# Placing SBUF buffers at multiples of 512 bytes, with a set offset for each block of weights

## The chip, the cores and the metric

The kernel runs on one core of a Trainium2 chip. The metric is the device time of one execution in microseconds (us); a number given for a kernel is the median of several executions. Within an execution, times are taken from the hardware profiler's trace, counted from the start of its span.

## The reference

One decoder layer for 256 tokens of width 1024, all in float32:

```python
h = rms_norm(x); proj = h @ w_in            # q, k, v | c_q, c_kv, k_r | 2 x 1024 gate columns
o_a = moba_attention(rope(q), rope(k), v) @ w_branch_a      # 8 heads x 64; at 256 tokens plain causal
q = rms_norm(c_q) @ w_uq; kv = rms_norm(c_kv) @ w_ukv       # low-rank attention, 8 heads, 64 + 32 rope
o_b = mla_attention(q, kv, rope(k_r)) @ w_branch_b
merged = sigmoid(g_a) * o_a + sigmoid(g_b) * o_b
x = x + rms_norm(merged @ w_out)
x = x + rms_norm(relu(rms_norm(x) @ w_up)**2 @ w_down)      # hidden width 4096
```

## The kernel before

Every float32 product is made of three TensorE matmuls in the type float32r: each operand is split into a high part (ACT copies it, rounded) and a low part (DVE subtracts), and `mm3` (lines 177 to 182) adds high x high, low x high and high x low into one PSUM tile. Line 179 issues the first of the three and line 182 the other two. The order of TensorE's instructions is the order of the program text; the other engines' order is set by the same text and a few explicit dependencies.

A matmul has two SBUF operands. The **stationary** one (128 columns, 512 bytes of each partition) is loaded into the array by a weight load, which the profile lists as PEld; the **moving** one (256, 288, 384 or 512 columns) streams through. In the trace a matmul stands as `out<-moving,stationary`. Two helpers use `mm3`:

- `a_chunk` (lines 265 to 277): the activations `xt` or `ct` are stationary and a block of weights moves, 512 columns as a rule. It makes q, k, v, and the latent projections cq (384 columns) and ckv (288).
- `b_tile` (lines 279 to 285): a block of weights is stationary, 128 columns at a time, and activations of 256 tokens move. It makes the gates (16 blocks `g{m}_{br}`, line 539), the branch projections (8 blocks `br{m}`, line 621) and the up projection (14 pairs `up{2i}`, lines 857 to 862). `nope` (line 564) does the same for the blocks uq and uk.

`unit` (line 162) loads one block of up to 1024 columns into a `raw` tile by a DMA of SP's queue, and splits it into the tiles `whi` and `wlo`, which rotate through 5 buffers each. In the second half `load` and `split` (lines 647 to 666) do the same with 2048 columns: tiles `u_hi`, `u_lo` for up, `t` or `b` for down.

The stages, in order of time: q, cq and ckv; k with the rotary work; v with the latent work; both attentions, woven with gate tiles; the branch projections `br`; the output projection `out` (`mix`, line 718, 96 matmuls with weights moving); the first part of up, with the split x1 stationary and `t` moving (line 765); then a loop over pairs (line 857) in which 48 matmuls of up alternate with 21 or 24 of down (`down`, line 846). Down's stationary operand is the squared activation, `m_hi` or `m_lo`, and its moving operand a block of 512 columns of `t`, `b` or `u`. Down has 204 matmuls on `t`, 99 on `b` and 60 on `u` (the last 24 with 256 columns).

Tiles come from pools that are stacked upwards from the low end of a partition's bytes, or (side="right") downwards from the high end, in the order in which they are first asked for. So the start of a tile follows from the sizes of those before it. In the program as built the starts, taken modulo 512, are these (all buffers of one name have the same remainder; a slice of 128 columns is 512 bytes and a step of 256 columns 1024, so slices keep the remainder):

```
tile                         before    after
xt_hi, xt_lo, x1_hi, x1_lo     320       0
whi, wlo (blocks of unit)      480       0 + the block's offset
o_hi, o_lo                     384       0
mg_hi, mg_lo, ct_hi, ct_lo     480       0
u_hi, u_lo                     480       0 + the block's offset
t_hi, t_lo                     320       0
b_hi, b_lo, m_hi, m_lo         480       0
```

The code that sets the position of a block of weights:

```python
hi = wts.tile([P, UNIT], F32R, name="whi", tag="whi")[:, :width]          # line 168
hi = mlp(f"{tag}h").tile([P, size], F32R, name=f"{tag}_hi", tag=f"{tag}h")[:, :n]   # line 651
```

The load of the first up block (`upA0`, line 665, in `mix`) goes into a `raw_u` buffer that lies where tiles of the attention half lay, so it waits for their last readers or writers.

Of the kernel before, what the change touches and what calls it, by code (L numbers as in the profile page):

```python
# [133 lines left out]
def block_kernel(ctx: ExitStack, tc: tile.TileContext, x, xt, pos_col, g_post_in, weights, out):  # L134
    nc = tc.nc
    table, _ = _block_table()

    keep = ctx.enter_context(tc.tile_pool(name="keep", bufs=1))

    first_half, attention_part = ExitStack(), ExitStack()  # L140
    late, wts = (first_half.enter_context(tc.tile_pool(name=n, bufs=b, side="right"))
# [17 lines left out]
    last_split = []  # L159


    def unit(key, hi=None, lo=None, behind=None):


        off, width = table[key]
        raw = wts.tile([P, UNIT], F32, name="raw", tag="raw", bufs=6)[:, :width]
        if hi is None:
            hi = wts.tile([P, UNIT], F32R, name="whi", tag="whi")[:, :width]
            lo = wts.tile([P, UNIT], F32R, name="wlo", tag="wlo")[:, :width]
        nc.sync.dma_start(raw, weights[off:off + P * width].rearrange("(p c) -> p c", c=width))  # L170
        ops = nc.scalar.activation(hi, raw, AF.Copy), nc.vector.tensor_tensor(lo, raw, hi, op=OP.subtract)  # L171
        for op, first in zip(ops, behind or ()):
            after(op, first)
        last_split[:] = ops
        return hi, lo

    def mm3(ps, a_hi, a_lo, b_hi, b_lo, first, last, a_lo_last=False):
# [22 lines left out]
    inv_freq = att.tile([P, 16], F32, name="inv_freq")  # L200
    for i in range(16):
        nc.gpsimd.memset(inv_freq[:, i:i + 1], INV_FREQ[i])
    mask = att.tile([P, 3 * P], F32, name="mask")
    nc.gpsimd.memset(mask, 0.0)
    for c in (0, 2):
        m = mask[:, c * P:(c + 1) * P]
        nc.gpsimd.affine_select(m, m, pattern=[[-1, P]], base=0, channel_multiplier=1,
                                compare_op=OP.is_ge, fill=NEG)


    stat = keep.tile([P, 128], F32, name="stat")
# [53 lines left out]
    def a_chunk(ps, key, n, x_hi, x_lo, nk, starts, before=None):  # L265

        starts = list(starts) + [nk]
        for k0, k1 in zip(starts, starts[1:]):
            if before is not None:
                before(k0, k1)  # L270
            hi, lo = (u.rearrange("p (k n) -> p k n", n=n) for u in unit(f"{key}{k0}"))
            for k in range(k0, k1):
                for t in range(NT):
                    tok = slice(t * P, (t + 1) * P)
                    mm3(ps[t], x_hi[:, k, tok], x_lo[:, k, tok], hi[:, k - k0], lo[:, k - k0],
                        k == 0, k == nk - 1)
                yield 6 * n / 2.4
# [25 lines left out]
    ctx.enter_context(tc.manual_schedule(engines={nc.tensor.engine}))  # L303


    zeros = att.tile([P, 512], BF16, name="zeros")
    nc.vector.memset(zeros, 0.0)
    first = stat_cols(1)
    nc.scalar.activation(first, zeros[:, :1], AF.Copy)
# [147 lines left out]
    def attention(br, products, v_of, scale):  # L457


        ranges = ((0, P), (P, 3 * P))  # L460
        probs, pts = {}, {}

        def softmax(h, sp):
            sm = att.tile([P, 3 * P], F32, name="sm", tag="sm", bufs=3)
            st = att.tile([P, 6], F32, name="st", tag="st", bufs=4)
            pr = att.tile([P, 3 * P], F32, name="pr", tag="pr", bufs=4)
            for t, (a, b) in enumerate(ranges):
                nc.vector.tensor_tensor_reduce(sm[:, a:b], sp[t], mask[:, a:b], scale=-scale, scalar=3.0e38,
                                               op0=OP.add, op1=OP.min, accum_out=st[:, t:t + 1])
                last_exp[0] = nc.scalar.activation(pr[:, a:b], sm[:, a:b], AF.Exp, bias=st[:, t:t + 1], scale=-1.0,  # L470
                                     accum_out=st[:, 2 + t:3 + t])
            nc.vector.reciprocal(st[:, 4:6], st[:, 2:4])
            for t, (a, b) in enumerate(ranges):
                nc.vector.tensor_scalar(pr[:, a:b], pr[:, a:b], st[:, 4 + t:5 + t], None, op0=OP.mult)
            probs[h] = pr

        def turned(h):
            pp = wk_tile()
            transposes(pp, [probs[h][:, c * P:(c + 1) * P] for c in range(3)])
            pts[h] = att.tile([P, 3 * P], F32, name="pt", tag="pt", bufs=3)  # L480
            nc.scalar.copy(pts[h], pp[:, :3 * P])
# [53 lines left out]
    def gate_tiles():  # L535
        for m in range(KD):
            ps = acc_tile()
            for br in range(2):
                yield from b_tile(ps[:, br * S:(br + 1) * S], unit(f"g{m}_{br}"), xt_hi, xt_lo, KD)
            nc.vector.tensor_tensor(gate(m), ps.rearrange("p (b s) -> p b s", b=2),  # L540
                                    rstd_row[:, None, :].to_broadcast([P, 2, S]), op=OP.mult)
            gates_done[0] += 1
# [7 lines left out]
    def latent_work():  # L550
# [25 lines left out]
            nc.scalar.copy(dst[:, 1:4:2], psv[64:128])  # L576

        for i in range(2):
            yield from nope(unit(f"uq{i}_0"), 256, 0, range(3), qMT[0:NOPE, 4 * i:4 * i + 4])
        u = unit("uk0")  # L580
        for i in range(2):
            yield from nope(u, 512, i, (3, 4), kMT[0:NOPE, 4 * i:4 * i + 4])
        ps = [acc_tile() for _ in range(NT)]
# [34 lines left out]
    gates_up_to(1)  # L618
    left = KD - gates_done[0]
    for m in range(KD):  # L620
        u = unit(f"br{m}")
        ps = wk_tile()
        for br in range(2):
            run(b_tile(ps[:, br * S:(br + 1) * S], u, o_hi[:, br], o_lo[:, br], 4, base=4 * br))
            sig = nc.scalar.activation(gate(m)[:, br], gate(m)[:, br], AF.Sigmoid, bias=col(B_GATE, br * KD + m))
            after(sig, last_exp[0])
        pr = att.tile([P, 2 * S], F32, name="mp", tag="mp", bufs=2)
        nc.vector.tensor_tensor(pr, ps, gate(m).rearrange("p b s -> p (b s)"), op=OP.mult)
        sm = att.tile([P, S], F32, name="ms", tag=("ra", "rb")[m % 2])
# [14 lines left out]

        return mlp0 if tag in ("raw_u", "raw_d", "th", "tl", "m0n", "r") else mlp1[0]

    def split(src, tag, behind=(), parts=1):

        n = src.shape[-1]
        size = {"b": 3 * 512}.get(tag, PAIR)  # L650
        hi = mlp(f"{tag}h").tile([P, size], F32R, name=f"{tag}_hi", tag=f"{tag}h")[:, :n]
        lo = mlp(f"{tag}l").tile([P, size], F32R, name=f"{tag}_lo", tag=f"{tag}l")[:, :n]
        for i in range(parts):
            c = slice(i * n // parts, (i + 1) * n // parts)
            ops = nc.scalar.activation(hi[:, c], src[:, c], AF.Copy), \  # L655
                nc.vector.tensor_tensor(lo[:, c], src[:, c], hi[:, c], op=OP.subtract)  # L656
# [61 lines left out]
    def mix():  # L718


        us = [unit(f"out{k}") for k in range(KD)]
        up_a[:] = [split(load(f"upA{k}", tag), "t") for k, tag in ((0, "u"), (4, "d"))]
        pieces = [[acc_tile() for n in range(2)] for t in range(NT)]

# [132 lines left out]
    for i in range(WARM // 2, n_pairs):  # L857
        ps = wk_tile()
        behind = {2: (turned[0, 1], turned[1, 0]), 3: (turned[1, 1],)}.get(i, ())
        w = split(load(f"up{2 * i}", "u"), "u", behind, max(len(behind), 1))  # L860
        for j in range(2):
            run(b_tile(ps[:, j * S:(j + 1) * S], w, x1_hi, x1_lo, KD, base=j * KD))
            if i == WARM // 2 and j == 0:
# [76 lines left out]
```

## Time and profile before

| | |
|---|---|
| median of 3 executions | 371.86 us (371.44 to 371.88) |
| the profiled execution | 371.55 us |
| its span, first to last instruction | 369.8 us |
| mean granted TensorE clock | 0.994 |
| busy in the span | PE 97%, PEld 87%, DVE 81%, ACT 67%, POOL 2% |

The profile is of one execution. PE is a busy time in which matmuls overlap each other, so a busy share of 97% does not say at what pace the matmuls go; the pace is the distance from one matmul's start to the next one's, called the gap below. DVE is VectorE, ACT ScalarE, POOL GpSimd, SP the engine that issues the DMAs.

### The profile page before, as it was taken

How to read it: one execution, taken by the hardware profiler on the slowest of the kernel's cores; microseconds unless marked ns; L12 is line 12 of the kernel's file. 1: busy time of each engine (PE TensorE's matmuls, PEld its weight loads, DVE VectorE, ACT ScalarE, POOL GpSimd, SP SyncE). 2: the span in 40 equal slices, each digit the busy share in tenths (PEclk: the TensorE clock that was granted, in tenths of full speed). 3: DMA queues.
4: the chain of work that ended last, by engine and by line, in shares of the span. 5: the costliest groups of instructions: out<-in, count | busy, mean ns of one | idle time of the engine just before them, and what ended most of it. 6: DMA issues, size and time to landing. Idle time of an engine off the chain costs nothing.

```text
span 369.8 us, 6081 instructions
## 1 busy us (share of the span) xinstructions
PE 359.7 (97%) x2319; PEld 321.5 (87%) x2319; DVE 298.0 (81%) x555; ACT 248.8 (67%) x375; POOL 6.5 (2%) x29
## 2 busy tenths in 40 slices
PE   8999999999999999999999999999999999999992
PEld 4699888989998999998879998889999888999881
DVE  4898898985766576796686999999989979978556
ACT  6889569996758755647289966767747766545422
POOL 6000000000000000000000000000000000000000
PEclk9999999999999999999999999999999999999997
DMA  7987763455434356574804756456564447330002
GB/s 252 403 327 244 258 205 106 125 218 152 136 96 133 113 172 178 179 268 179 334 3 165 268 194 252 180 193 228 228 217 161 170 177 284 131 115 0 2 0 113
DMA packets 15036, 66.20 MB, mean 179 GB/s; under 512 B 1696, under 2 KB 2208, under 8 KB 10912
## 3 DMA queue, kind: packets, MB, share of 16 engines
q1 hardware_dynamic: 14688, 65.30, 50.5%
q10 hardware_dynamic: 288, 0.52, 0.4%
q8 instruction: 18, 0.29, 0.3%
q14 instruction: 10, 0.08, 0.1%
q0 software_dynamic: 32, 0.00, 0.0%
HBM read 64.77 MB, written 1.05 MB: 178 GB/s over the span
## 4 chain that ended last, share of the span: by engine, by line
PE 91%; DVE 4%; DMA 2%; ACT 1%; SPq 1%; issue 1%; DVEq 0%; ACTq 0%
PE acc L182 30%; PE wk L182 27%; PE acc L179 15%; PE wk L179 13%; PE wk L368 3%; DMA raw<-in_weights 2%; PE wk L488 1%; PE wk L520 1%; ACT sq L242 1%; DVE y L898 1%; PE wk L489 1%; DVE x_lo L714 0%; PE wk L519 0%; SPq L255 0%; DVE y L685 0%
## 5 line engine op out<-in xcount | busy, mean ns | idle before, releaser
L171 DVE TENSOR_TENSOR wlo<-raw,whi 128x1024 fp32r<-128x1024 f32 (+4 forms) x58 | 65.7, 1139 | 20.3 <-ACT whi L171 20.3
L171 ACT ACTIVATE whi<-raw 128x1024 fp32r<-128x1024 f32 (+4 forms) x58 | 57.2, 992 | 28.6 <-PE acc L182 13.3
L179 PE MATMUL wk<-x_hi,u_hi 128*128 128x256 f32 x224 | 63.3, 283 | 0.0
L182 PE MATMUL wk<-x_lo,u_hi 128*128 128x256 f32 x224 | 63.3, 282 | 0.0
L182 PE MATMUL wk<-x_hi,u_lo 128*128 128x256 f32 x224 | 62.9, 281 | 0.0
L655 ACT ACTIVATE u_hi<-raw_u 128x2048 fp32r<-128x2048 f32 (+1 forms) x17 | 30.9, 1816 | 28.0 <-PE wk L182 27.9
L656 DVE TENSOR_TENSOR u_lo<-raw_u,u_hi 128x2048 fp32r<-128x2048 f32 (+1 forms) x17 | 36.8, 2162 | 10.6 <-ACT u_hi L655 10.2
L182 PEld LDWEIGHTS wk<-x_lo,u_hi 128*128 128x128 f32 x224 | 42.1, 188 | 0.6
L182 PEld LDWEIGHTS wk<-x_hi,u_lo 128*128 128x128 f32 x224 | 42.5, 190 | 0.0
L179 PEld LDWEIGHTS wk<-x_hi,u_hi 128*128 128x128 f32 x224 | 42.0, 187 | 0.6
L179 PE MATMUL acc<-xt_hi,whi 128*128 128x256 f32 x128 | 37.8, 295 | 0.0
L182 PE MATMUL acc<-xt_hi,wlo 128*128 128x256 f32 x128 | 36.1, 282 | 0.0
L182 PE MATMUL acc<-xt_lo,whi 128*128 128x256 f32 x128 | 36.0, 281 | 0.0
L656 DVE TENSOR_TENSOR t_lo<-t,t_hi 128x2048 fp32r<-128x2048 f32 x11 | 25.2, 2288 | 2.0 <-ACT t_hi L655 1.9
L805 ACT ACTIVATE m_hi<-m 128x896 fp32r<-128x896 f32 (+1 forms) x16 | 14.6, 917 | 15.9 <-DVE m L801 13.6
L179 PEld LDWEIGHTS acc<-xt_hi,whi 128*128 128x128 f32 x128 | 24.0, 188 | 1.1 <-issue 1.0
L182 PEld LDWEIGHTS acc<-xt_lo,whi 128*128 128x128 f32 x128 | 24.2, 189 | 0.1
L182 PEld LDWEIGHTS acc<-xt_hi,wlo 128*128 128x128 f32 x128 | 24.1, 188 | 0.0
L655 ACT ACTIVATE t_hi<-t 128x2048 fp32r<-128x2048 f32 x11 | 21.0, 1911 | 1.8 <-PE acc L182 1.1
L656 DVE TENSOR_TENSOR b_lo<-raw_d,b_hi 128x1536 fp32r<-128x1536 f32 x11 | 19.2, 1749 | 0.0
L806 DVE TENSOR_TENSOR m_lo<-m,m_hi 128x896 fp32r<-128x896 f32 (+1 forms) x16 | 16.6, 1044 | 2.5 <-ACT m_hi L805 2.5
L182 PE MATMUL acc<-t_lo,m_hi 128*128 128x512 f32 x46 | 18.3, 398 | 0.0
(254 smaller groups left out, 927.9 us busy)
## 6 DMA issues: line engine op xcount, KB each, us to landing
raw<-in_weights SPq DMA_DIRECT2D x44, 512.0 KB, 3.6
raw_u<-in_weights SPq DMA_DIRECT2D x17, 1024.0 KB, 5.0
raw_d<-in_weights SPq DMA_DIRECT2D x15, 1024.0 KB, 4.9
raw<-in_weights SPq DMA_DIRECT2D x7, 384.0 KB, 6.9
raw<-in_weights SPq DMA_DIRECT2D x4, 256.0 KB, 4.5
x_sb<-in_x SPq DMA_DIRECT2D x2, 512.0 KB, 8.1
g_post<-in_g_post SPq DMA_DIRECT2D x2, 512.0 KB, 5.4
raw<-in_weights SPq DMA_DIRECT2D x2, 432.0 KB, 6.8
```

The lines of the kernel that those rows point to most:

```text
L171: ops = nc.scalar.activation(hi, raw, AF.Copy), nc.vector.tensor_tensor(lo, raw, hi, op=OP.subtract)
L179: nc.tensor.matmul(ps, a_hi, b_hi, start=first, stop=False)
L182: nc.tensor.matmul(ps, a, b, start=False, stop=last and i == 1)
L242: return nc.scalar.activation(sq[:, :src.shape[-1]], src, AF.Square, scale=scale, accum_out=accum)
L368: nc.tensor.transpose(ps[:n, i * P:(i + 1) * P], b, ident)
L488: nc.tensor.matmul(o[:, 0:S], v_of(0, h), pts[h][:, 0:S], start=True, stop=False)
L489: nc.tensor.matmul(o[:, P:S], v_of(1, h), pts[h][:, S:S + P], start=False, stop=True)
L520: nc.tensor.matmul(sp[:, P:3 * P], q[:, P:2 * P], k, start=True, stop=True)
L655: ops = nc.scalar.activation(hi[:, c], src[:, c], AF.Copy), \
L656: nc.vector.tensor_tensor(lo[:, c], src[:, c], hi[:, c], op=OP.subtract)
L805: nc.scalar.activation(hi, m[:, used], AF.Copy)
L806: nc.vector.tensor_tensor(lo, m[:, used], hi, op=OP.subtract)
```

## The change

Three things are done. The large tiles are moved to multiples of 512 bytes, by fillers (`edge`, `pad_kr`, `pad_o`, a wider `stat`) and by letting small tiles share buffers (`zeros` with `rb`, `mp` with `sm`; `mask` loses a third, since both score ranges can read the same causal block). The tiles of weights get 512 bytes more, and each block starts at its own offset in them: a gate block at 32(2m+br) bytes, a k block at 64 k0, a v block at 64 k0 + 64, an out block at 32(2k+1), an up block at 32 i, the blocks br, uq and uk at 192; all others at 0. The arguments `hi`, `lo` and `behind` of `unit`, which no call used, are gone.

```diff
+ROW, SKEW = 512, 192
+    ctx.enter_context(tc.tile_pool(name="edge", bufs=1, side="right")).tile([P, 120], F32, name="edge")
-    def unit(key, hi=None, lo=None, behind=None):
+    def unit(key, skew=0):
         off, width = table[key]
         raw = wts.tile([P, UNIT], F32, name="raw", tag="raw", bufs=6)[:, :width]
-        if hi is None:
-            hi = wts.tile([P, UNIT], F32R, name="whi", tag="whi")[:, :width]
-            lo = wts.tile([P, UNIT], F32R, name="wlo", tag="wlo")[:, :width]
+        hi, lo = (wts.tile([P, UNIT + ROW // 4], F32R, name=n, tag=n)[:, skew // 4:skew // 4 + width]
+                  for n in ("whi", "wlo"))
...
-    mask = att.tile([P, 3 * P], F32, name="mask")
+    mask = att.tile([P, 2 * P], F32, name="mask")
-    for c in (0, 2):
-        m = mask[:, c * P:(c + 1) * P]
-        nc.gpsimd.affine_select(m, m, ...
+    nc.gpsimd.affine_select(mask[:, P:], mask[:, P:], ...
-    stat = keep.tile([P, 128], F32, name="stat")
+    stat = keep.tile([P, 176], F32, name="stat")
-            hi, lo = (... for u in unit(f"{key}{k0}"))
+            hi, lo = (... for u in unit(f"{key}{k0}", 64 * k0 + 64 * (key == "v") if key in "kv" else 0))
-    zeros = att.tile([P, 512], BF16, name="zeros")
+    zeros = att.tile([P, 512], BF16, name="zeros", tag="rb")
+    att.tile([P, 48], F32, name="pad_kr")
+    att.tile([P, 64], F32, name="pad_o")
-                nc.vector.tensor_tensor_reduce(sm[:, a:b], sp[t], mask[:, a:b], ...
+                nc.vector.tensor_tensor_reduce(sm[:, a:b], sp[t], mask[:, 2 * P - (b - a):], ...
-                yield from b_tile(ps[:, br * S:(br + 1) * S], unit(f"g{m}_{br}"), xt_hi, xt_lo, KD)
+                yield from b_tile(ps[:, br * S:(br + 1) * S], unit(f"g{m}_{br}", 32 * (2 * m + br)), xt_hi, xt_lo, KD)
-            yield from nope(unit(f"uq{i}_0"), ...
-        u = unit("uk0")
+            yield from nope(unit(f"uq{i}_0", SKEW), ...
+        u = unit("uk0", SKEW)
-        u = unit(f"br{m}")
+        u = unit(f"br{m}", SKEW)
-        pr = att.tile([P, 2 * S], F32, name="mp", tag="mp", bufs=2)
+        pr = att.tile([P, 2 * S], F32, name="mp", tag="sm", bufs=3)
-    def split(src, tag, behind=(), parts=1):
+    def split(src, tag, behind=(), parts=1, skew=0):
-        size = {"b": 3 * 512}.get(tag, PAIR)
-        hi = mlp(f"{tag}h").tile([P, size], F32R, ...)[:, :n]
-        lo = mlp(f"{tag}l").tile([P, size], F32R, ...)[:, :n]
+        size = {"b": 3 * 512, "u": PAIR + ROW // 4}.get(tag, PAIR)
+        hi = mlp(f"{tag}h").tile([P, size], F32R, ...)[:, skew // 4:skew // 4 + n]
+        lo = mlp(f"{tag}l").tile([P, size], F32R, ...)[:, skew // 4:skew // 4 + n]
-        us = [unit(f"out{k}") for k in range(KD)]
+        us = [unit(f"out{k}", 32 * (2 * k + 1)) for k in range(KD)]
-        w = split(load(f"up{2 * i}", "u"), "u", behind, max(len(behind), 1))
+        w = split(load(f"up{2 * i}", "u"), "u", behind, max(len(behind), 1), 32 * i)
```

No instruction changes its place on PE, ACT, DVE or SP; POOL has one AFFINE_SELECT less at its start. Two DMAs wait for something else, because the buffers now lie over other tiles of the first half. On SP's queue, at the end of `mix`'s loads, stood before:

```order
L170 DMA raw<-in_weights 128x1024 [waits DMAHW5_49,DVE_49]
L665 DMA raw_u<-in_weights 128x2048 [waits PE_49,Pool_49]
L665 DMA raw_d<-in_weights 128x2048 [waits PE_49]
L665 DMA raw_u<-in_weights 128x2048 [waits DMAHW6_49,DVE_49,Pool_49]
L665 DMA raw_u<-in_weights 128x2048 [waits DMAHW7_49,DMAHW4_49,DVE_49]
```

and with the change:

```order
L171 DMA raw<-in_weights 128x1024 [waits DMAHW5_49,DVE_49]
L663 DMA raw_u<-in_weights 128x2048 [waits DVE_49,PE_49,Pool_49]
L663 DMA raw_d<-in_weights 128x2048 [waits PE_49]
L663 DMA raw_u<-in_weights 128x2048 [waits DMAHW6_49,Pool_49]
L663 DMA raw_u<-in_weights 128x2048 [waits DMAHW7_49,DMAHW4_49,DVE_49]
```

The first `raw_u` is upA0. It now waits also for DVE, and the count it waits for is that of the last `mg_lo` (m = 7, line 632 before). The third load, up4, no longer waits for DVE (a count reached three DVE steps earlier, at the last `mp`).

## Rows read from the trace of the kernel before

**Rows 1.** The page: busy time, share of the span and instructions of each engine, and the chain that ended last by engine.

```profile
PE 359.7 (97%) x2319; PEld 321.5 (87%) x2319; DVE 298.0 (81%) x555; ACT 248.8 (67%) x375; POOL 6.5 (2%) x29
PE 91%; DVE 4%; DMA 2%; ACT 1%; SPq 1%; issue 1%; DVEq 0%; ACTq 0%
```

**Rows 2.** The waits of PE over the whole span: who waited for whom, us in total, times, longest us.

```profile
PE wk L312 <- DVE stat L636: 1.3, 1, 1.3
PE acc L182 <- DVE x_lo L714: 0.9, 1, 0.9
PE wk L182 <- DVE wlo L171: 0.5, 1, 0.5
PE wk L179 <- ACT whi L171: 0.2, 1, 0.2
```

**Rows 3.** Three stretches: start and end, us, busy us (and instructions) of PE, PEld, DVE, ACT, POOL, granted PE clock, DMA share, GB/s.

```profile
0.00:20.00 20.00, 18.02 (x64) 11.85 (x65) 13.12 (x27) 14.47 (x23) 6.47 (x29) 1.00 0.90 333
220.00:240.00 20.00, 20.00 (x130) 18.10 (x129) 19.74 (x19) 14.10 (x12) 0.00 (x0) 1.00 0.59 215
280.00:300.00 20.00, 20.00 (x134) 18.37 (x133) 17.43 (x17) 12.81 (x11) 0.00 (x0) 1.00 0.60 211
```

**Rows 4.** The timeline of PE in one turn of the loop over pairs: start us, duration us, instruction. The first and last of 12 matmuls of down on t, of 48 of up, and of 9 of down on b.

```profile
246.35 0.40 PE L179 MATMUL acc<-t_hi,m_hi 128*128 128x512 f32 x1
...
248.93 0.40 PE L182 MATMUL acc<-t_lo,m_hi 128*128 128x512 f32 x1
249.17 0.28 PE L179 MATMUL wk<-x_hi,u_hi 128*128 128x256 f32 x1
...
254.81 0.28 PE L182 MATMUL wk<-x_hi,u_lo 128*128 128x256 f32 x1
254.92 0.39 PE L179 MATMUL wk<-b_hi,m_hi 128*128 128x512 f32 x1
...
256.78 0.39 PE L182 MATMUL acc<-b_lo,m_hi 128*128 128x512 f32 x1
```

**Rows 5.** The same view: the first and the last three of 48 matmuls of a gate tile.

```profile
135.47 0.28 PE L179 MATMUL acc<-xt_hi,whi 128*128 128x256 f32 x1
...
140.87 0.28 PE L179 MATMUL acc<-xt_hi,whi 128*128 128x256 f32 x1
140.98 0.29 PE L182 MATMUL acc<-xt_lo,whi 128*128 128x256 f32 x1
141.11 0.28 PE L182 MATMUL acc<-xt_hi,wlo 128*128 128x256 f32 x1
```

**Rows 6.** The same view: the first and last of 120 matmuls of the branch projections br3 to br7.

```profile
149.47 0.28 PE L179 MATMUL wk<-o_hi,whi 128*128 128x256 f32 x1
...
163.44 0.28 PE L182 MATMUL wk<-o_hi,wlo 128*128 128x256 f32 x1
```

**Rows 7.** The same view: the first of the out projection, its 60th (the first to use the low part of block out7), and its 93rd, the last before transposes come between.

```profile
163.55 0.39 PE L179 MATMUL acc<-whi,mg_hi 128*128 128x512 f32 x1
...
176.93 0.39 PE L182 MATMUL acc<-wlo,mg_hi 128*128 128x512 f32 x1
...
184.41 0.39 PE L182 MATMUL acc<-wlo,mg_hi 128*128 128x512 f32 x1
```

**Rows 8.** The same view, near the end of the loop: the first and last of 36 matmuls of down on u.

```profile
351.36 0.40 PE L179 MATMUL acc<-u_hi,m_hi 128*128 128x512 f32 x1
...
359.33 0.39 PE L182 MATMUL acc<-u_lo,m_hi 128*128 128x512 f32 x1
```

**Rows 9.** The same view: the first and last of 48 matmuls each of cq (384 columns), ckv (288) and k (512).

```profile
18.75 0.34 PE L179 MATMUL acc<-whi,xt_hi 128*128 128x384 f32 x1
...
26.89 0.34 PE L182 MATMUL acc<-wlo,xt_hi 128*128 128x384 f32 x1
27.07 0.29 PE L179 MATMUL acc<-whi,xt_hi 128*128 128x288 f32 x1
...
33.33 0.30 PE L182 MATMUL acc<-wlo,xt_hi 128*128 128x288 f32 x1
33.46 0.40 PE L179 MATMUL wk<-whi,xt_hi 128*128 128x512 f32 x1
...
44.48 0.39 PE L182 MATMUL wk<-wlo,xt_hi 128*128 128x512 f32 x1
```

**Rows 10.** The timeline of DVE around the load of upA0: the last mg_lo, and the low parts of upA0 and of block out7.

```profile
165.96 0.42 DVE L632 TENSOR_TENSOR mg_lo<-ms,mg_hi 128x256 fp32r<-128x256 f32 x1
...
171.92 2.29 DVE L656 TENSOR_TENSOR t_lo<-raw_u,t_hi 128x2048 fp32r<-128x2048 f32 x1 [0.58 <-ACT t_hi L655]
174.13 1.22 DVE L171 TENSOR_TENSOR wlo<-raw,whi 128x1024 fp32r<-128x1024 f32 x1
```

**Rows 11.** The timeline of SP's queue: the issues of upA0 and upA4.

```profile
158.15 0.38 SPq L665 DMA_DIRECT2D raw_u<-in_weights  x1
163.63 0.33 SPq L665 DMA_DIRECT2D raw_d<-in_weights  x1
```

**Rows 12.** All loads of line 665 in the span: time from issue to landing.

```profile
DMA to landing us min/median/max: 4.7/4.9/7.3
```

**Rows 13.** The timeline of ACT: the high parts of upA0 and of out7.

```profile
169.98 1.90 ACT L655 ACTIVATE t_hi<-raw_u 128x2048 fp32r<-128x2048 f32 x1
171.79 1.05 ACT L171 ACTIVATE whi<-raw 128x1024 fp32r<-128x1024 f32 x1
```

More of the change, by code (lines that the diff above doesn't have):

```diff
@@ L159, in block_kernel @@
     last_split = []
-    def unit(key, hi=None, lo=None, behind=None):
+    def unit(key, skew=0):
         off, width = table[key]
         raw = wts.tile([P, UNIT], F32, name="raw", tag="raw", bufs=6)[:, :width]
-        if hi is None:
-            hi = wts.tile([P, UNIT], F32R, name="whi", tag="whi")[:, :width]
-            lo = wts.tile([P, UNIT], F32R, name="wlo", tag="wlo")[:, :width]
+        hi, lo = (wts.tile([P, UNIT + ROW // 4], F32R, name=n, tag=n)[:, skew // 4:skew // 4 + width]
+                  for n in ("whi", "wlo"))
         nc.sync.dma_start(raw, weights[off:off + P * width].rearrange("(p c) -> p c", c=width))
[L171 to L174, printed above, removed]
+        last_split[:] = nc.scalar.activation(hi, raw, AF.Copy), nc.vector.tensor_tensor(lo, raw, hi, op=OP.subtract)
         return hi, lo
@@ L202, in block_kernel @@
         nc.gpsimd.memset(inv_freq[:, i:i + 1], INV_FREQ[i])
-    mask = att.tile([P, 3 * P], F32, name="mask")
+    mask = att.tile([P, 2 * P], F32, name="mask")
     nc.gpsimd.memset(mask, 0.0)
-    for c in (0, 2):
-        m = mask[:, c * P:(c + 1) * P]
-        nc.gpsimd.affine_select(m, m, pattern=[[-1, P]], base=0, channel_multiplier=1,
-                                compare_op=OP.is_ge, fill=NEG)
-    stat = keep.tile([P, 128], F32, name="stat")
+    nc.gpsimd.affine_select(mask[:, P:], mask[:, P:], pattern=[[-1, P]], base=0, channel_multiplier=1,
+                            compare_op=OP.is_ge, fill=NEG)
+    stat = keep.tile([P, 176], F32, name="stat")
     used = [0]
@@ L270, in a_chunk @@
                 before(k0, k1)
-            hi, lo = (u.rearrange("p (k n) -> p k n", n=n) for u in unit(f"{key}{k0}"))
+            hi, lo = (u.rearrange("p (k n) -> p k n", n=n) for u in unit(f"{key}{k0}", 64 * k0 + 64 * (key == "v") if key in "kv" else 0))
             for k in range(k0, k1):
@@ L467, in softmax @@
             for t, (a, b) in enumerate(ranges):
-                nc.vector.tensor_tensor_reduce(sm[:, a:b], sp[t], mask[:, a:b], scale=-scale, scalar=3.0e38,
+                nc.vector.tensor_tensor_reduce(sm[:, a:b], sp[t], mask[:, 2 * P - (b - a):], scale=-scale, scalar=3.0e38,
                                                op0=OP.add, op1=OP.min, accum_out=st[:, t:t + 1])
@@ L578, in latent_work @@
         for i in range(2):
-            yield from nope(unit(f"uq{i}_0"), 256, 0, range(3), qMT[0:NOPE, 4 * i:4 * i + 4])
-        u = unit("uk0")
+            yield from nope(unit(f"uq{i}_0", SKEW), 256, 0, range(3), qMT[0:NOPE, 4 * i:4 * i + 4])
+        u = unit("uk0", SKEW)
         for i in range(2):
@@ L645, in mlp @@
         return mlp0 if tag in ("raw_u", "raw_d", "th", "tl", "m0n", "r") else mlp1[0]
-    def split(src, tag, behind=(), parts=1):
+    def split(src, tag, behind=(), parts=1, skew=0):
         n = src.shape[-1]
-        size = {"b": 3 * 512}.get(tag, PAIR)
-        hi = mlp(f"{tag}h").tile([P, size], F32R, name=f"{tag}_hi", tag=f"{tag}h")[:, :n]
-        lo = mlp(f"{tag}l").tile([P, size], F32R, name=f"{tag}_lo", tag=f"{tag}l")[:, :n]
+        size = {"b": 3 * 512, "u": PAIR + ROW // 4}.get(tag, PAIR)
+        hi = mlp(f"{tag}h").tile([P, size], F32R, name=f"{tag}_hi", tag=f"{tag}h")[:, skew // 4:skew // 4 + n]
+        lo = mlp(f"{tag}l").tile([P, size], F32R, name=f"{tag}_lo", tag=f"{tag}l")[:, skew // 4:skew // 4 + n]
         for i in range(parts):
```

## The prediction

> **What bounds the kernel now.** I read the page first: PE is busy for 97% of the span and holds 91% of the chain that ended last [rows 1]. Then the waits of PE: all that PE waits for on other engines is 2.9 us, 1.3 of it before the first matmul [rows 2]. So from about 20 us on the time is the number of matmuls times the gap from one start to the next; before that the loads have a say (PE 18.02 of 20 us, DMA 0.90) [rows 3]. The granted clock is 1.00, the upper of its two levels, 2.4 GHz, in these stretches [rows 3], so no gap below is long because of the clock. The third reading is therefore the gap itself, from the first and last start of a run of matmuls.
>
> At 2.4 GHz 256 columns take 106.7 ns, 384 take 160.0, 512 take 213.3. The gaps are longer, and not all by the same amount. Up: 5.64 us over 47 gaps, 120.0 ns, 13.3 over [rows 4]. Gates: again 5.64 over 47, 120.0 [rows 5]. br: 13.97 over 119, 117.4, only 10.7 over [rows 6]. With 512 columns: out 20.86 over 92, 226.7 or 13.4 over [rows 7]; down on u 7.97 over 35, 227.7 or 14.4 over [rows 8]; down on b 1.86 over 8, 232.5 or 19.2 over; down on t 2.58 over 11, 234.5 or 21.2 over [rows 4]; k 11.02 over 47, 234.5 or 21.2 over [rows 9]. cq is 8.14 over 47, 173.2 or 13.2 over, and ckv (288 columns, 120.0) 6.26 over 47, 133.2 or 13.2 over [rows 9].
>
> While a matmul streams its moving operand, the stationary operand of the next one is loaded. I call **residue** the start of what is being loaded minus the start of what moves, modulo 512. From the table of starts it is, before: 160 for up, gates and t; 96 for br; 0 for out, u, b, uq and uk; 352 for k, v and cq; 96, 224 and 352 in turn for ckv. The gaps differ by residue at equal width (96 against 160 at 256 columns, 0 against 160 and 352 at 512), which is the only sign in this trace that placement counts; b, at 0 but slow, shows that it is not all.
>
> **The change, part by part.** Instructions, their order and their sizes stay on PE, DVE and ACT, so what can change is the gap, stage by stage, and the two waits on SP's queue.
>
> *Gates and up* (384 + 672 = 1056 matmuls) leave residue 160 and go through all sixteen (gates) and fourteen (up) multiples of 32. The nearest readings at widths up to 384 are an excess of 10.7 at residue 96, 13.3 at 160 and 13.2 for cq and ckv; their mean 12.4 gives 119.1 ns, 0.9 less than now: -0.95 us. No row shows the other residues. The far bounds are single gaps, 0.11 and 0.13 us within one gate tile [rows 5], which would be -10.6 and +10.6 if every residue were as its best or worst gap; readings over whole runs, 117.4 and 120.0, bound it by -2.7 and 0, and they are nearer, since single gaps alternate within one residue.
>
> *Down on t* (204) goes from residue 160 to 0. At 0 stand out and u (226.7, 227.7) and b (232.5). t shares m with both; I take 230: -4.5 ns, -0.9 us, between -1.6 and -0.4. *b* and *u* keep their residue: 0, though b may come to u's gap (99 x -4.8, -0.5).
>
> *out* (96) leaves the best reading, 226.7 at residue 0, for the odd multiples of 32, 160 and 352 among them (234.5). I take 232: +0.5 us, between 0 and +0.75. *k and v* (96) leave 234.5 for all multiples of 64, 0 among them; 232 gives -0.25, between -0.75 and 0.
>
> *br* (192) goes from 96 to 192. With the same 119.1 it loses 1.7 ns: +0.3 us, between -0.8 (113 ns) and +0.5 (120.0).
>
> *q, cq, ckv, uq, uk*: q runs where loads limit it [rows 3]; cq and ckv have the usual 13.2; 60 matmuls of uq and uk go from residue 0 to 192. Together 0, give or take 0.2.
>
> *The load of upA0* waits for the last mg_lo, which ends at 165.96 + 0.42 = 166.38 [rows 10]; it is issued at 158.15 now [rows 11]. With 4.9 us to land [rows 12] it is there at 171.3, and ACT's t_hi, at 169.98 now [rows 13], starts 1.3 us later. Behind it on ACT stands whi of out7, and on DVE t_lo and then wlo of out7, which ends at 174.13 + 1.22 = 175.35 now [rows 10] and then at about 176.65. Its first reader is the 60th matmul of out, at 176.93, whose weights and columns are fetched about one gap earlier, 176.7 [rows 7]. So it just holds, and with out at 232 the reader comes 59 x 5.3 = 0.3 us later: 0. If the load takes the longest 7.3, wlo is 2.4 us later and PE stands for 2 us. upA4 is issued behind it, at 166.8 and not 163.63 [rows 11], and has longer to its first reader. POOL's missing instruction and up4's dropped wait free nothing that PE waits for.
>
> *DVE* is busy for 19.74 of 20 us in one stretch of the loop and 17.43 in another [rows 3]; a loop turn that PE makes 0.1 us shorter still fits on average.
>
> The sum: -0.95 - 0.9 + 0.5 - 0.25 + 0.3 = -1.3 us. The profiled execution of 371.55 becomes 370.25; it lies 0.3 under the median of 371.86, which becomes 370.6.
>
> **A rule that speaks against it.** The gap of up is 120.0 and that of t 234.5 [rows 4], and br, with the width of up, has 117.4 [rows 6]. The Trainium skill, "TensorE: Matmul & The Clock Gate", section "Step-by-step: what each phase is for", says that PE has two independent SBUF read ports, so that loading the next weights takes nothing from the running matmul. By that page's "Back-to-back issue gap", N/2.4 + 2.5 ns, up would have 109.2 (an estimate from the page), and no placement could change it. The rows speak against the letter of it, as the excess is 10.7 to 21.2 and not 2.5; what it would mean here is the second case below.
>
> **The cases.** A difference over 0.2%, 0.74 us, is what a measurement of this kernel can tell from none.
>
> 1. As summed, 370.6: 45%. It can miss by a microsecond either way and then ends within 0.2% about one time in four.
> 2. Placement makes no difference; what differs between stages is something else that goes with them (the order of operands, the banks written, how a run begins). For it: b and u differ by 5 ns at one residue, and cq has 13.2 at the residue at which k has 21.2. Against it: t and u share width, helper and m. Time 371.9: 18%. That the change then does nothing is also what the rule above would say.
> 3. Some residues are much better than any seen. If a third of gates and up came to 113 ns, that is 352 x 7 = -2.5 in place of -0.95: 369.0. For it: gaps of 0.11 occur [rows 5]. Against it: no run of matmuls has an excess under 10.7. 15%.
> 4. Slower: at some residues 256 columns pay what 512 pay at 160 and 352, some 7.3 ns more than the usual excess. At four of sixteen that is 264 x 7.3 = +1.9 in place of -0.95, and the sum is +1.6: 373.5. It decides once the mean over the swept residues is over 121.0 ns, that is, from three such residues on. For it: 21.2 is seen at two of the four residues that 512 columns have. Against it: up has 13.3 at one of them. 14%.
> 5. The wait of upA0 bites for half a microsecond or more, in out, on the 60th matmul: 371.1 to 372.6 with the rest as summed. 8%.
>
> Faster by over 0.2%: three quarters of case 1, all of 3 and a little of 5, 0.53. Within: the rest of 1, 2 and most of 5, 0.32. Slower: 4 and the edges, 0.15. The range from 368.2 to 372.8 takes in cases 1 to 3 and 5 and the milder half of 4; outside it stay a case 3 with half of the residues good and a case 4 with four or more bad ones, under 2 in 10.
>
> **What would show it.** The sixteen gate tiles should have gaps that differ from one another and repeat at the same offset in up; t should fall to 227 to 232; out should lose its steady 226.7; br stay between 117 and 120. Case 2 is shown by gates and up at 120.0 throughout and t at 234.5. The wait of upA0 would show as idle time of PE before a matmul of out with DVE's wlo as its releaser. The sum is wrong if the mean over gates and up lies outside 117.4 to 121, or if DVE stops PE in the loop.

## The result, and the profile after

The changed kernel takes 368.29 us (median of 4 runs, 368.13 to 368.68), against 371.81 for the kernel before on the same chip: a ratio of 0.9909, 95% interval 0.9892 to 0.9926. So it is faster by 3.4 us, where 1.3 was forecast; the 368.29 us lie 0.1 above the lower end of the forecast range, 368.2. The profiled execution took 368.18 us with a span of 366.5.

The page of after answers to [rows 1]; PE is as full as before and holds the same share of the chain:

```profile
PE 356.5 (97%) x2319; PEld 319.8 (87%) x2319; DVE 297.8 (81%) x555; ACT 248.9 (68%) x375; POOL 6.1 (2%) x28
PE 91%; DVE 4%; DMA 2%; ACT 1%; SPq 1%; issue 1%; DVEq 0%; ACTq 0%
```

The waits of PE after answer to [rows 2]; they total 2.7 us, against 2.9:

```profile
PE wk L308 <- DVE stat L634: 1.3, 1, 1.3
PE acc L180 <- DVE x_lo L712: 0.9, 1, 0.9
PE wk L180 <- DVE wlo L172: 0.5, 1, 0.5
```

The windows after answer to two of [rows 3] (same columns). PE has no idle time in them and the clock is 1.00 again, its upper level; DVE, at 20.00 of 20 us, is now full in one of them, yet PE does not wait for it:

```profile
220.00:240.00 20.00, 20.00 (x132) 18.29 (x131) 20.00 (x20) 14.19 (x13) 0.00 (x0) 1.00 0.62 227
280.00:300.00 20.00, 20.00 (x136) 18.43 (x135) 17.90 (x17) 12.52 (x11) 0.00 (x0) 1.00 0.59 211
```

So the 3.3 us of span are in the gaps. The timeline of PE after shows, each time by its first and last matmul: 48 of k; a gate block at offset 416 (24); br3 to br7 (120); out (93); the up pair i = 4 at offset 128 (48); a loop turn with 12 of t, 48 of up i = 7 at offset 224, and 9 of b; and 36 of u:

```profile
32.98 0.39 PE L177 MATMUL wk<-whi,xt_hi 128*128 128x512 f32 x1
...
43.81 0.40 PE L180 MATMUL wk<-wlo,xt_hi 128*128 128x512 f32 x1
...
136.72 0.28 PE L177 MATMUL acc<-xt_hi,whi 128*128 128x256 f32 x1
...
139.47 0.29 PE L180 MATMUL acc<-xt_hi,wlo 128*128 128x256 f32 x1
...
148.07 0.28 PE L177 MATMUL wk<-o_hi,whi 128*128 128x256 f32 x1
...
162.09 0.28 PE L180 MATMUL wk<-o_hi,wlo 128*128 128x256 f32 x1
162.21 0.39 PE L177 MATMUL acc<-whi,mg_hi 128*128 128x512 f32 x1
...
183.62 0.39 PE L180 MATMUL acc<-wlo,mg_hi 128*128 128x512 f32 x1
...
216.15 0.29 PE L177 MATMUL wk<-x_hi,u_hi 128*128 128x256 f32 x1
...
221.80 0.29 PE L180 MATMUL wk<-x_hi,u_lo 128*128 128x256 f32 x1
...
244.97 0.39 PE L177 MATMUL acc<-t_hi,m_hi 128*128 128x512 f32 x1
...
247.46 0.40 PE L180 MATMUL acc<-t_lo,m_hi 128*128 128x512 f32 x1
247.69 0.28 PE L177 MATMUL wk<-x_hi,u_hi 128*128 128x256 f32 x1
...
253.18 0.28 PE L180 MATMUL wk<-x_hi,u_lo 128*128 128x256 f32 x1
253.29 0.40 PE L177 MATMUL wk<-b_hi,m_hi 128*128 128x512 f32 x1
...
255.13 0.39 PE L180 MATMUL acc<-b_lo,m_hi 128*128 128x512 f32 x1
...
348.03 0.39 PE L177 MATMUL acc<-u_hi,m_hi 128*128 128x512 f32 x1
...
355.96 0.39 PE L180 MATMUL acc<-u_lo,m_hi 128*128 128x512 f32 x1
```

Read as before, last start minus first, over the gaps between: k 10.83/47 = 230.4 ns (234.5 in [rows 9]); the gate block 2.75/23 = 119.6 (120.0 in [rows 5]); br 14.02/119 = 117.8 (117.4 in [rows 6]); out 21.41/92 = 232.7 (226.7 in [rows 7]); up i = 4 5.65/47 = 120.2 and i = 7 5.49/47 = 116.8 (120.0 in [rows 4]); t 2.49/11 = 226.4 and b 1.84/8 = 230.0 (234.5 and 232.5 in [rows 4]); u 7.93/35 = 226.6 (227.7 in [rows 8]).

For the whole kernel I added, from the same starts, the time from each matmul's start to the next one's, by stage (us). The last two columns are two of the experiments below, and the last row takes in PE's other work, transposes and attention:

| stage | forecast | before | after | change | all at 0 | chosen offsets |
|---|---|---|---|---|---|---|
| up | (with gates) -0.95 | 80.65 | 79.67 | -0.98 | 80.62 | 78.29 |
| gates | | 47.84 | 47.22 | -0.62 | 47.81 | 46.22 |
| down on t | -0.9 | 47.78 | 46.39 | -1.39 | 46.32 | 46.33 |
| q, k, v (512 columns) | (k, v) -0.25 | 36.91 | 36.45 | -0.46 | 36.26 | 36.44 |
| down on b | 0 | 22.92 | 22.72 | -0.20 | 22.72 | 22.54 |
| br | +0.3 | 22.59 | 22.61 | +0.02 | 23.04 | 22.41 |
| out | +0.5 | 21.87 | 22.43 | +0.56 | 21.91 | 21.88 |
| uq, uk | 0 | 7.46 | 7.35 | -0.11 | 7.44 | 7.26 |
| all of PE | -1.3 | 361.05 | 357.69 | -3.36 | 359.12 | 354.57 |

By residue, the mean gap over up blocks of after is (ns): 64: 115.9, 96: 120.0, 128: 120.1, 160: 119.9, 192: 117.8, 224: 116.7, 256: 119.8, 288: 118.3, 320: 117.8, 352: 117.3, 384: 120.1, 416: 119.9, 448: 117.8, 480: 116.7. The 115.9 at 64 is a mean of two: transposes cut this pair in half, and the gap is 117.8 ahead of them and 113.3 soon behind them. Gates have 115.2 at 64 and 116.7 to 119.6 elsewhere, and not always what up has at the same offset: the last gate block, at 480, has 117.9.

The load of upA0 after, on SP's queue, and DVE around it, answering to [rows 10, 11]:

```profile
165.12 0.33 SPq L663 DMA_DIRECT2D raw_u<-in_weights  x1
```

```profile
164.61 0.42 DVE L630 TENSOR_TENSOR mg_lo<-ms,mg_hi 128x256 fp32r<-128x256 f32 x1
...
174.22 1.22 DVE L172 TENSOR_TENSOR wlo<-raw,whi 128x1024 fp32r<-128x1024 f32 x1
```

The issue does wait for the last mg_lo, which ends at 165.03. That is 1.35 us earlier than in [rows 10], since the stages ahead of it got shorter, so wlo of out7 is ready at 175.44, before the 60th matmul of out starts at 175.97.

### The profile page after: what moved, and what is told of

Read it like the earlier page. It is cut to its first block, busy times and chain, and to the rows that moved or that the text cites. A ratio compares the mean times of both kernels' runs of the same rounds, so it can differ in the third digit from the quotient of the medians.

```text
span 366.5 us, 6079 instructions
## 1 busy us (share of the span) xinstructions
PE 356.5 (97%) x2319; PEld 319.8 (87%) x2319; DVE 297.8 (81%) x555; ACT 248.9 (68%) x375; POOL 6.1 (2%) x28
## 4 chain that ended last, share of the span: by engine, by line
PE 91%; DVE 4%; DMA 2%; ACT 1%; SPq 1%; issue 1%; DVEq 0%; ACTq 0%
PE acc L180 30%; PE wk L180 27%; PE acc L177 15%; PE wk L177 13%; PE wk L365 3%; DMA raw<-in_weights 2%; PE wk L486 1%; PE wk L518 1%; ACT sq L238 1%; DVE y L896 1%; PE wk L487 1%; DVE x_lo L712 0%; PE wk L517 0%; SPq L251 0%; DVE y L683 0%
## 5 line engine op out<-in xcount | busy, mean ns | idle before, releaser
L653 ACT ACTIVATE b_hi<-raw_d 128x1536 fp32r<-128x1536 f32 x11 | 16.3, 1484 | 3.4 <-DMA raw_d<-in_weights 3.4
```

## The experiments

Theory: the gap of a stage follows from where its two operands start in their 512 bytes, so each stage has its own term. Rivals: the aligned buffers as such, or something that goes with the stages (order, banks, neighbours). A pair is the 48 matmuls of one up block, and the entry of a run is what PE did just before it. Offsets are those given to `unit` and `split`; "gates g" stands for the argument in `gate_tiles`, "up u" for that in the loop over pairs.

**Alignment alone.** All offsets 0, buffers as in the change:

```diff
-ROW, SKEW = 512, 192
+ROW, SKEW = 512, 0
-  gates 32 * (2 * m + br), up 32 * i, out 32 * (2 * k + 1), k and v 64 * k0 ...
+  gates 0, up 0, out 0, k and v 0
```

> Alignment alone: every block at offset 0, buffers at multiples of 512. Theory 1 (residue): up, gates and br go to the gap of residue 0, 119.8 (+1.0, +0.6, +0.4 us), out to 226.7 (-0.6), k and v to 228.5 (-0.3); t keeps 227.2: about 369.4 us, so alignment gives 2.4 of the 3.5 us, most of it in t. Rival, starting at a multiple of 512 is itself what is fast, and the offsets only cost: 368.3 or less.

Measured 369.54 us, ratio 0.9948 [0.9934, 0.9963] to before. In the table t and q, k, v gain as in the change or more, out loses nothing, up and gates stay where they were, and br, now at 0, loses 0.45 us. In the timeline of PE, up i = 7:

```profile
248.49 0.28 PE L177 MATMUL wk<-x_hi,u_hi 128*128 128x256 f32 x1
...
254.12 0.28 PE L180 MATMUL wk<-x_hi,u_lo 128*128 128x256 f32 x1
```

5.63/47 = 119.8 ns, where the change has 116.8. So about 1.9 us of the change come from the common start, and the offsets add the rest, which is their gain in up, gates and br minus their loss in out. Most of the 1.9 is in t. No kernel here puts t back at residue 160 with the rest of the change kept, so that t's part is due to its starts is argued from this: its matmuls changed in nothing else but the starts of what runs ahead of them, and PE waits for nothing there.

**The same differences at other starts.** All large tiles are moved 160 bytes, so that no start is a multiple of 512 but every residue stays:

```diff
-    stat = keep.tile([P, 176], F32, name="stat")
+    stat = keep.tile([P, 216], F32, name="stat")
-    ... .tile([P, 120], F32, name="edge")
+    ... .tile([P, 208], F32, name="edge")
```

> The changed kernel with every tile 160 bytes past a multiple of 512, so that all residues between tiles stay and no tile is aligned. Theory 1 (only the difference of the starts counts): 368.3 us within 0.5, t at 227, the gaps of up by offset as before (64 at 116, 96 and 128 at 120, 192 at 117.8). Rival, the start of each operand by itself counts (alignment to 512): t goes back to 234 (+1.4 us), the table by offset shifts by 160, and the time goes towards 371.

Measured 368.34 us (368.32 to 368.62), ratio 0.9918 [0.9901, 0.9935]: the time of the change, with the gap of each up pair the same to 0.1 ns. Multiples of 512 play no part; the difference of starts does. This also refutes the second case of the prediction: between this kernel, the one at 0 and the changed one nothing differs but starts, and up moves by 0.95 us, gates by 0.6 and out by 0.5 when the differences do, and by 0.03 or less when they are kept.

**One good residue everywhere.** Gates, up, br, uq, uk at 64, the rest at 0:

```diff
-ROW, SKEW = 512, 192
+ROW, SKEW = 512, 64
-  gates 32 * (2 * m + br), up 32 * i, out 32 * (2 * k + 1), k and v 64 * k0 ...
+  gates 64, up 64, out 0, k and v 0
```

> All 256-column stages with weights loaded (gates, up, br, uq, uk) at offset 64, all 512-column stages (k, v, out) at 0. Theory 1, the residue between what is loaded and what moves sets the gap: gates and up come from a mean of 118.2 to about 115.7 ns (1056 x -2.5 = -2.6 us), br from 117.8 to 115.7 (-0.4), out from 232.8 to 226.7 (-0.6), k and v from 231.8 to 228.5 (-0.3): about 364.4 us. Rival, the differences between the offsets are chance of each tile (its buffer, how its run begins) and no property of the offset: the mean stays near 118.2 and the time near 368.3, with out alone worth -0.6.

Measured 365.91 us, ratio 0.9851 [0.9836, 0.9866]: about 2.2 us better than the change (the difference of the ratios to before, and of PE's time in the traces), 1.5 short of the expectation. The timeline of PE shows what is missing. Pair i = 3 and pair i = 4, same offset, same buffers:

```profile
203.56 0.28 PE L177 MATMUL wk<-x_hi,u_hi 128*128 128x256 f32 x1
...
208.88 0.28 PE L180 MATMUL wk<-x_hi,u_lo 128*128 128x256 f32 x1
...
214.46 0.28 PE L177 MATMUL wk<-x_hi,u_hi 128*128 128x256 f32 x1
...
220.00 0.28 PE L180 MATMUL wk<-x_hi,u_lo 128*128 128x256 f32 x1
```

5.32/47 = 113.2 ns and 5.54/47 = 117.9. Within a run the gaps repeat: 113, 113, 114 in the one, 118, 118, 117, 119 and the like in the other, to the end of the run. Pair 3 follows a half pair that begins after transposes; pair 4 and all later ones begin after down. So one residue has two stable patterns, and the entry into the run may choose between them.

**Finer steps.** Gates at 16(2m + br), up at 16(i + 14):

```diff
-  gates 32 * (2 * m + br), up 32 * i
+  gates 16 * (2 * m + br), up 16 * (i + 14)
```

> Offsets in steps of 16 bytes: gates at 0 to 240, up at 256 to 464. Theory 1 with a period of 256: gates and up agree where the offsets agree modulo 256; offset 64 is the best of the multiples of 32 (115.4) and the neighbours 48 and 80 tell how wide it is: a unit of 32 bytes would make 64 and 80 equal, a smooth curve puts them between 115 and 120. Rival, period 512 or none: up at 320 stays near 117.8 while gates have 115.4 at 64. The time is 367 to 369.5 us with either.

One run: 368.44 us. Gates had 114.3 ns at 64 but 118.6 at 80 and 117.8 at 48; gates had 116.7 at 208 and up 116.6 at 464. 32 bytes are not the unit.

**Period.** The offsets of the former moved by 256, and odd ones for out, k, v:

```diff
-  gates 32 * (2 * m + br), up 32 * i, out 32 * (2 * k + 1), k and v 64 * k0 ...
+  gates 256 + 16 * (2 * m + br), up 16 * (i - 2), out 16 * (2 * k + 1), k and v 256 + 16 * (k0 + 1), v another 128
```

> As the change, with other offsets: up blocks at 16 x (i - 2), 0 to 208; gates at 256 + 16 x (2m + br); out at 16 x (2k + 1); k and v at 256 + 16 x (k0 + 1), v another 128 on. If the gap repeats every 256 bytes at 256 columns, up at an offset x gives what the change gave at x + 256 (119.8 ns at 0, 118.4 at 16, 117.8 at 64, 116.6 at 208) and gates at 320 what it gave at 64 (114 to 115 ns). If it repeats only every 512 bytes, up at 0 to 208 differs from that by a ns or more and gates at 320 stay at 116.6. About 368 us either way.

One run: 368.16 us. Up at 16, 64, 208 had 118.4, 117.8, 116.7 ns, as at 272, 320, 464 in the run before; gates had 114.2 at 320 and 116.7 at 464, as at 64 and 208. All 14 up pairs had the gap of the run before to 0.1 ns. The pair at 208 in PE's timeline:

```profile
332.89 0.28 PE L177 MATMUL wk<-x_hi,u_hi 128*128 128x256 f32 x1
...
338.37 0.28 PE L180 MATMUL wk<-x_hi,u_lo 128*128 128x256 f32 x1
```

5.48/47 = 116.6 ns. At 256 columns the gap repeats every 256 bytes.

**Which stationary operand counts?** The low halves are moved another 64 bytes, so that the operand loaded next keeps residue 64, while a matmul's own is at 64, 0 and 128 in turn:

```diff
-        hi, lo = (wts.tile(...)[:, skew // 4:skew // 4 + width] for n in ("whi", "wlo"))
+        hi, lo = (wts.tile(...)[:, (skew + d) // 4:(skew + d) // 4 + width]
+                  for n, d in (("whi", 0), ("wlo", 64)))
```

(with the same for `u_lo`, and fillers that put `xt_lo` and `x1_lo` at 64)

> As the kernel with gates and up blocks at 64, but the lo halves (of the weights and of the activations alike) are moved another 64 bytes, so that each pass changes which start is compared with which. By the theory that what counts is the stationary operand loaded for the next matmul against the running matmul's moving operand, residues stay 64 through nearly all of gates and up: 113 to 118 ns, about 366 us. By the rival that a matmul's own stationary and moving operands are compared, the three passes stand at residues 64, 0 and 128: about 118.5 to 120 ns, up and gates 1,080 x 1.5 = about 1.6 us more, 367.5 us.

One run: 368.78 us. Up and gates took 79.69 + 47.35 us, 1.7 more than with 64 throughout; out, whose `wlo` moved as well, took 0.46 more. Up i = 7 in PE's timeline:

```profile
248.02 0.28 PE L177 MATMUL wk<-x_hi,u_hi 128*128 128x256 f32 x1
...
253.59 0.28 PE L180 MATMUL wk<-x_hi,u_lo 128*128 128x256 f32 x1
```

5.57/47 = 118.5 ns, in a repeating pattern of 9 gaps from 115 to 124 that is neither of those of residue 64. So what is loaded next, set against what moves, is not what counts alone. The 118.5 fits the rival, a matmul's own pair of starts, but does not prove it: here the starts of successive moving operands differ too, as do those of successive stationary ones, which they do in no other kernel. In all other kernels a matmul's own difference and that to the next load are the same within a run, so they can't separate the two.

**Does the entry choose the pattern?** As with 64 throughout, with a transpose of 128 columns ahead of br0 and of the up pairs from i = 4 on:

```diff
         ps = wk_tile()
+        if i > BEHIND:
+            nc.tensor.transpose(ps[:, :P], ident, ident)
```

> The kernel with gates and up blocks at 64, the rest at 0, plus one transpose of 128 columns on PE ahead of the first br tile and ahead of each up tile from the fifth on (i = 4 to 15), 13 transposes in all, which write the tile's PSUM region before the tile's own first matmul overwrites it. With the blocks at 64 alone the up tiles ran at 117.8 ns a matmul from the first down tile on, and at 113.3 ns in the two tiles that follow the eight transposes of the second residual's rows; the starts were the same in both. Theory that the pattern of gaps depends on how a run is entered: after a transpose the up tiles run at about 113.4 ns, which is 520 x 4.4 ns = 2.3 us less, for about 13 x 0.115 = 1.5 us of transposes, and br may gain as well: about 363.6 to 365 us. Rival, that something other than the entry (the PSUM region, the work of other engines) sets it: 365.9 + 1.5 = 367.4 us, up at 117.8.

Measured 366.00 us, ratio 0.9851 [0.9834, 0.9867]: between the two. The timeline of PE at pair i = 7, and then at i = 8:

```profile
245.62 0.40 PE L180 MATMUL acc<-t_lo,m_hi 128*128 128x512 f32 x1
245.85 0.27 PE L860 MATMUL wk<-ident 128*128 128x128 f32 x1
245.88 0.36 PE L177 MATMUL wk<-x_hi,u_hi 128*128 128x256 f32 x1
246.08 0.28 PE L180 MATMUL wk<-x_lo,u_hi 128*128 128x256 f32 x1
...
246.67 0.28 PE L177 MATMUL wk<-x_hi,u_hi 128*128 128x256 f32 x1
...
251.32 0.28 PE L180 MATMUL wk<-x_hi,u_lo 128*128 128x256 f32 x1
...
256.45 0.28 PE L180 MATMUL wk<-x_lo,u_hi 128*128 128x256 f32 x1
...
257.04 0.28 PE L177 MATMUL wk<-x_hi,u_hi 128*128 128x256 f32 x1
```

In pair 7 the rows 246.67 to 251.32 are 41 gaps of 113.4 ns; in pair 8 five gaps take 0.59 from the second matmul on, 118 each, and it stays so. Of 12 pairs 8 ran at 113.3 after the first few matmuls and 4 at 117.8 (i = 4, 8, 11 and 14); br stayed at 117.8. The starts of the operands are those of the kernel without the transposes, where all 12 pairs had 117.8, so the entry has a say; but the same transpose came ahead of all 12, so it does not decide alone. The gain was spent on the transposes: from the last of t to the second of up it is 0.46 us here and 0.35 without (0.11 each).

**Shorter breaks.** On the version of the last experiment below, but with up at 64, first a transpose of 16 rows and columns, then an fp32 matmul of 128 rows and 16 columns, ahead of each up pair from i = 4 on:

```diff
+            nc.tensor.transpose(ps[:, :16], ident[:16], ident[:16, :16])
```

> As the version chosen from the gaps, but up at 64 throughout, with a transpose of 16 columns (instead of 128) ahead of each up tile from i = 4 on. The 128-column transposes cost about 0.11 us each and put 8 of 12 tiles on the 113.3 ns pattern. If the short one costs half and locks as many: 8 x 48 x 3.4 ns = 1.3 us less and 4 x 48 x 1.1 = 0.2 more than at 208, and 0.6 us for the transposes: about 364.4 us. If it costs as much as the long one: 365.1. If it locks none: 365.0 + 0.6 + 0.6 = about 366.1 us.

```diff
+            nc.tensor.matmul(ps[:, :16], ident, ident[:, :16], start=True, stop=True)
```

> As the version chosen from the gaps (364.6 us), but up at 64 throughout, with one fp32 matmul of the identity on its own first 16 columns (128 rows, 128 x 16) ahead of each up tile from i = 4 on, which the tile's own first matmul overwrites. The transpose of 16 columns by 16 rows put all 12 tiles on the 113.3 ns pattern but cost 0.35 us each, since its 16-row weights were not loaded ahead of the running matmul; the 128-column transpose cost 0.11 us and locked 8. Theory that any break of the run can lock it and that 128-row weights are loaded ahead: about 0.06 us each, 12 x 48 x 3.4 ns = 1.95 us less in up than at 208, 0.7 us for the extra matmuls: about 363.4 us if all 12 lock, 364.2 if 8 do. If none locks: 364.6 + 0.65 + 0.7 = 366.0 us. If it costs what the transpose of 16 rows did: about 366.8.

Measured 367.59 us, ratio 0.9895 [0.9879, 0.9912], and 368.09, 0.9908 [0.9892, 0.9925]. The first put all 12 pairs on 113.3 ns, the second none. PE at pair 7 in the first:

```profile
245.58 0.39 PE L180 MATMUL acc<-t_lo,m_hi 128*128 128x512 f32 x1
245.90 0.23 PE L858 MATMUL wk<-ident 16*128 16x16 f32 x1
246.05 0.39 PE L177 MATMUL wk<-x_hi,u_hi 128*128 128x256 f32 x1
246.28 0.28 PE L180 MATMUL wk<-x_lo,u_hi 128*128 128x256 f32 x1
```

and in the second:

```profile
245.63 0.39 PE L180 MATMUL acc<-t_lo,m_hi 128*128 128x512 f32 x1
245.86 0.29 PE L858 MATMUL wk<-ident 128*128 128x16 f32 x2
246.00 0.36 PE L177 MATMUL wk<-x_hi,u_hi 128*128 128x256 f32 x1
246.20 0.28 PE L180 MATMUL wk<-x_lo,u_hi 128*128 128x256 f32 x1
```

From the last of t to the second of up: 0.70 and 0.57 us, 0.35 and 0.22 more than without. The second is two instructions of PE in the profile (x2). A break that puts every pair on the faster pattern was found, a cheap one was not. What in the entry decides (8 of 12, all, none) stays open.

**Steps of 4 and 8 bytes.**

```diff
+  up (200, 204, 212, 216, 220, 224, 228, 232, 48, 56, 60, 68)[i - 4], br 176 + 8 * m, late gates 196 to 220
```

> Offsets in steps of 4 and 8 bytes around the two good places: up tiles i = 4 to 15 at 200, 204, 212, 216, 220, 224, 228, 232, 48, 56, 60, 68; br tiles m = 0 to 7 at 176 to 232 in steps of 8; the late gates at 196, 200, 204, 212, 220. If the gap depends on starts in units of 16 bytes or more, neighbours within such a unit have equal gaps (208 and 212 116.7 ns; 60 as 48, 118.4). If it depends on each 4-byte element, they differ by a ns or more, and one of them may be below 116.7 ns. About 365.5 us either way.

One run: 366.89 us. In PE's timeline the pairs at 204 and at 224:

```profile
225.07 0.28 PE L177 MATMUL wk<-x_hi,u_hi 128*128 128x256 f32 x1
...
230.85 0.29 PE L180 MATMUL wk<-x_hi,u_lo 128*128 128x256 f32 x1
...
268.03 0.28 PE L177 MATMUL wk<-x_hi,u_hi 128*128 128x256 f32 x1
...
273.51 0.28 PE L180 MATMUL wk<-x_hi,u_lo 128*128 128x256 f32 x1
```

5.78/47 = 123.0 and 5.48/47 = 116.6 ns. 212 gave 117.3, 216 119.6, 60 119.6 and 68 118.4: every 4-byte element counts, none of the new ones is better than 208, and a careless offset is worse than any the change uses.

**Offsets chosen from the gaps.** 64 where a run is entered well, 208 elsewhere, 0 for k, v, out:

```diff
-  gates 32 * (2 * m + br), up 32 * i, br SKEW, uq and uk 192, out 32 * (2 * k + 1), k and v 64 * k0 ...
+  gates 64 if 2 * m + br < 11 else 208, up 64 if i < 4 else 208, br 208, uq and uk 64, out 0, k and v 0
```

> Offsets chosen from the gaps measured so far: 64 where a run is entered so that it locks at 113 to 114 ns (the eleven gate tiles before the first br tile, the up tiles i = 2 and 3, uq and uk), 208 in the other gates, in br and in up from i = 4 on (116.7 ns at 208 in two kernels, against 117.8 at 64 there), 0 for k, v and out. Against the kernel with 64 everywhere (365.91 us): up 12 x 48 x 1.1 ns = 0.63 us less, br 192 x 1.1 = 0.21 less, five gate tiles 120 x 1.1 = 0.13 less: about 364.9 us. If 208 works only at the two places where it was measured, br gives nothing: 365.1 to 365.3. If the gap at 208 was an accident of what ran ahead of it there, no gain: 365.9.

Measured 364.61 us (364.58 to 365.05), ratio 0.9817 [0.9803, 0.9832] to before, the best of all. Up i = 7 in PE's timeline:

```profile
245.44 0.28 PE L177 MATMUL wk<-x_hi,u_hi 128*128 128x256 f32 x1
...
250.92 0.28 PE L180 MATMUL wk<-x_hi,u_lo 128*128 128x256 f32 x1
```

5.48/47 = 116.6 ns, as in all 12 pairs after down. br and the late gates too have 116.7 (gates take 46.22 us in the table, and took 46.41 with 64 throughout), so at 208 one pattern was met from every entry tried.

## Why the prediction was right, and where its sizes were off

The mechanism held in the main: no instruction moved on PE, the waits stayed, and the gaps changed stage by stage as the starts did. The direction of each large term was right. Two parts of it did not hold as written. The residue was defined by what is loaded while a matmul runs, and the kernel with moved low halves shows that this does not count alone. And the gaps were to repeat at the same offset in gates and up, which they do only where the entry leads to the same pattern (117.8 in both at 448, but 117.9 and 116.7 at 480). What fell short were sizes, by 2 us together. The forecast of 370.6 was 2.3 us too high, more than the microsecond that case 1 allowed for, and the range, 368.2 to 372.8, was wide for other cases; that it holds 368.29 is in part luck.

The terms, in us:

- *Gates and up*, -0.95 forecast, -1.60 measured. The step that failed is the assumed mean of 119.1 ns over the swept residues, taken from br at 96, up at 160 and the excess of cq and ckv. Over all of them it is 118.3; 96 and 160 themselves are among the slow ones (120.0 and 119.9), and with br's 117.4 in [rows 6] beside up's 120.0, 96 too has had two gaps.
- *Down on t*, -0.9 forecast, -1.39 measured: I took 230 between b's 232.5 and u's 226.7 to 227.7; it is 227.2 over the stage, near u's 226.6. b was a poor guide because its gap hangs on its entry: in after, a run of down behind an up pair has two to nine gaps between 224 and 238 ns before it settles near 226.7, and b's runs end after 9 matmuls. With its own starts unchanged, b has 227.9 ns behind the pair at 192, 231.4 behind that at 128, and 226.6 in its last run, which follows t. In before that last run had 231.5, behind t at 234. The -0.20 of b fits this.
- *br*, +0.3 forecast, +0.02 measured, for the same 119.1; at 192 it is 117.8. *uq and uk*, 0 forecast, gained 0.11. *k and v* gained 0.23, as forecast (-0.25). The other 0.23 in their row is q's, forecast at 0, and not the work of the starts: in the kernels above whose q blocks start at 0, q takes from 13.5 to 14.0 us, against 13.97 before, and there the loads limit PE [rows 3].
- *out*, +0.5 forecast, +0.56 measured, and shown by its removal: at 0 it has 21.91 us again.
- *upA0's wait* cost nothing, as forecast, with 0.5 us from the end of `wlo` to its reader's start. The forecast let the reader's columns be fetched a gap ahead of that start; where PE did wait for a `wlo`, early in before, its matmul started 0.05 us after DVE's end, so there was more room than reckoned.

Of the rivals, the second (placement makes no difference) is refuted by the kernels above, which differ in starts alone. The rule weighed there, from the Trainium skill, "TensorE: Matmul & The Clock Gate", section "Step-by-step: what each phase is for", would have left the gap the same whatever the starts; at one width and order, with the granted clock at 1.00, its upper level, the pairs ran from 113.2 to 123.0 ns as starts and entry changed. Whether it is the load of the next weights that slows the running matmul is not shown. The third has a part in the result: residue 64 gave 115.2 to 115.9, with stretches of 113.3, but only at one of the sixteen offsets; at 320, the same residue by the period of 256, up had 117.8. The fourth, four slow residues with 7.3 ns more, did not occur: the slowest of the sweep has 120.1.

## What to carry to other kernels

Where PE is full, compare the gap of one matmul with another of the same width before looking for work to remove: here 1.8% of the time lay in where operands start. Align what shares a stage so that the difference of starts is 0 or a measured good value, measure over whole runs and in the place where they run, and prefer an offset that is good from every entry (208) to one that is best from some (64). A sweep over all offsets, as in the change, buys the mean of them; its use is to find the good ones, and a stage that is at its best already, as out was, should be left out of it.

## What the hardware showed that was not expected

- The gap of a float32r matmul depends on the difference between the starts of its operands, in steps of 4 bytes, with a period of 256 bytes at 256 columns: 113.2 to 123.0 ns over a pair. With 512 columns it was 226.6 to 234.5.
- Runs settle into short repeating patterns, and one residue can hold two (113.3 and 117.8 at 64), depending on what ran just before, down to a b run of 9 matmuls whose gap (226.6 to 231.9 in after) follows what ran ahead of it.
- A 16-row transpose between 128-row matmuls cost 0.35 us and an fp32 matmul of 128 rows and 16 columns (two instructions of PE) 0.22, both more than a transpose of 128 columns (0.11).
